# A two-layer hybrid block on one core: rows of v summed by column-quarter products, gates of both layers built through DRAM

## The chip, the cores and the metric

The kernel runs on one core of a Trainium2 chip. The metric is the device time of one execution in microseconds. Three runs of the kernel before are shown.

## What is computed

A block of two layers over 256 latent tokens and 256 context tokens of width 1024. Each layer mixes tokens (a gated delta rule in chunks, pooling, a Fourier mix), adds the result, and then retrieves experts. Context tokens go through the same weights, see only the context, and stop after the scan of the second layer. The change touches the retrieval:

```python
def _peer(h, w_query, sub_keys, expert_u, expert_v):
    ...
    best, pos = lax.top_k(cand.reshape(t, PEER_HEADS, PEER_TOPK * PEER_TOPK), PEER_TOPK)
    idx = jnp.take_along_axis(cand_idx..., pos, axis=-1)
    gate = jax.nn.softmax(best, axis=-1)
    ...
        act = jax.nn.gelu(jnp.einsum('td,thkd->thk', hb, expert_u[ib]), approximate=False)
        wgt = gb * act
        return jnp.einsum('thk,thkd->td', wgt, expert_v[ib])
```

Each token has 8 heads x 16 chosen experts of 16384 (128 x 128 keys). A chosen expert's row of u gives a score, its row of v is added with the weight gate times gelu(score).

## The kernel before

**Order of the work.** `_body` issues the parts in program order, and a scheduler of the tile framework then sets each engine's order; every engine works its own list strictly in that order. SP issues the loads of weights and tables, POOL the indirect fetches. The parts are: layer 0 of the context (`columns`, `scan`, `modulation`, `update`, `gather_select`), the latents of layer 0 (`columns`, `scan`, `update`, `dense_select`), the stream of layer 0, and layer 1 of the latents the same way. The second layer's scan of the context is `context()`, given to the stream of layer 0 for tile KV = 114.

**Two ways of retrieval.** For the latents all experts are worked out for all tokens (`stream`, line 1087). A tile is one first key, 128 experts. `first(i)` loads a tile of u, splits it in two parts (`hu` by ScalarE at line 1100, `lu` by POOL at line 231) and makes 24 products of 256 columns (lines 1111 to 1113); ScalarE applies gelu. `second(i)`, 17 tiles later in layer 0 and 32 later in layer 1, loads the tile of v, splits it (`hv`, and `lv` on VectorE at line 1101), multiplies the weights by the gates (line 1131), splits them too (`wh`, and `wl` on POOL in layer 0, on VectorE in layer 1), and makes 12 products of 512 columns (line 1142) into four banks.

**Gates.** They must lie as [second key, first key, token]. In layer 1 `build` (line 1059) makes one-hot masks of both keys for two tokens at a time (line 1070, VectorE), multiplies one by the gate (POOL or ScalarE), multiplies the two on TensorE (line 1082), and writes them to DRAM in 16 pieces of 1 MB; `second` reads 1 MB for every 8 tiles. In layer 0 `chunk` (line 1028) makes them within the stream, 32 first keys at a time: masks `two`, `one`, `og` on VectorE (lines 1037, 1041, 1046), and three bf16 products of 32 columns per token (line 1052).

**Rows of the context's experts.** For the context of layer 0 only the chosen rows are fetched. `gather_rows` (line 956) takes choice j of a block of 128 tokens: one indirect DMA from POOL brings [128, 2048], each token's row of u and of v side by side (line 966, 1 MB). VectorE multiplies the u half by the token and sums it (line 975, and every seventh later one on POOL and ScalarE), ScalarE makes the weight (lines 979, 980), and VectorE adds the v half times the weight (line 986). There are 256 such fetches, four buffers for the first 100 and three after. The first 100 are issued ahead of the latents of layer 0, the others by `context()`:

```python
    fetching = gather_rows(0, CTX, m, rows, buffer, chosen)
    for _ in range(UVN):
        next(fetching)
...
    sums = stream(0, keys, Hh, Hl, su, sv, LAG[0], {KV: context})
```

`modulation(0, (5,))` stands between scan and update of the latents; a vector of it is 16 products whose outputs are a quarter of the columns each, in groups of four side by side (`tile_position`), and 4.2 MB of weights.

Of the kernel before, what the change touches and what calls it, by code (L numbers as in the profile page):

```python
# [10 lines left out]
BF = mybir.dt.bfloat16  # L11
# [17 lines left out]
def _constants():  # L29
# [4 lines left out]
    # cumulative sums along the tokens of a chunk, forwards and backwards: [j, i]  # L34
# [5 lines left out]
    # masks are added to exponents' arguments: [token, token], nothing outside a chunk  # L40
# [55 lines left out]
def _layout(i):  # L96
# [25 lines left out]
    for l in range(depth):  # L122
# [22 lines left out]
def _body(st, tc, a, out, dbg, until):  # L145
# [26 lines left out]
    # the banks of PSUM: three for projections, one for each of three chains, two that sum outputs  # L172
# [3 lines left out]
    KC, TC = 32, 8  # first keys of a chunk of gates, tokens at a time  # L176
# [14 lines left out]
    class Stage:  # L191
        """tiles of a pool that is opened and closed by hand"""
# [11 lines left out]
    def bank(shape, tag):  # L204
        tag = roles.get(tag, tag)
        if tag == "pj":
# [26 lines left out]
    def rsqrt(x, n, tag=""):  # L233
        """1 / sqrt(x) of [128, n] positive values, by Newton's steps."""
# [10 lines left out]
    def two_parts(x, hi, lo):  # L245
        """x as a sum of two parts that the tensor engine reads exactly in one pass each"""
# [4 lines left out]
    def product(out, x, y, start, stop):  # L251
        """out += x^T y, of operands in one part, or in two: only the product of the two second ones drops out"""
# [4 lines left out]
    def wtile(name, *index):  # L257
        """2048 of a weight's columns as two tiles; a function of a row of 128 and the columns' width"""
# [43 lines left out]
    def scales(l, which, m, s):  # L302
        """norm's weight times 1 + scale, and the shift: [128, 8] each"""
# [4 lines left out]
    def in_rows(vec, half, tag):  # L308
        """half of [128, 8] as a row of 512, the same on all partitions"""
# [10 lines left out]
    def normed(x, xn, tag, scratch=None):  # L320
        """xn = x / rms(x), by rows"""
# [7 lines left out]
    def transposed(xns, sc, sh, hT):  # L329
        """hT [128, 8, 256] = (xn * sc + sh) transposed"""  # L330
# [16 lines left out]
    def columns_by_feature(name, c, hs):  # L347
        """256 columns of a weight times hT: [128, 2, 256], a column per partition"""
# [10 lines left out]
    def columns_by_token(name, n, h):  # L359
        """512 columns of a weight times hT: a block's [128, 512] each, a token per partition"""  # L360
# [33 lines left out]
    spots = cp.tile([128, NKEYS, TC], BF, tag="spots", name="spots")  # L394
    dve.tensor_copy(spots, iota[:, :, None].to_broadcast([128, NKEYS, TC]))
# [9 lines left out]
    def columns(l, s, m, full, keep, tl):  # L405
# [4 lines left out]
        else:  # the last use of X  # L410
# [13 lines left out]
        # gates of the delta rule: [token, block, 16]  # L424
# [16 lines left out]
        # softplus(z) = max(z, 0) + ln(1 + exp(-|z|))  # L441
# [24 lines left out]
        # factors by token: [beta, -beta exp(g), exp(g_end - g)]  # L466
# [6 lines left out]
        # decay of a whole chunk, on all partitions: [chunk, 8]  # L473
# [13 lines left out]
        def conv(part, hp):  # L487
            """silu of the short convolution for two heads: part 0, 1, 2 = q, k, v: [128, 2, 256]"""
# [814 lines left out]
```

## Time and profile before

| what | us |
|---|---|
| three runs: median, lowest, highest | 3429.58, 3420.82, 3435.34 |
| the profiled execution: its span, the one time that the page gives of it | 3421.3 |
| busy in it: TensorE products / weight loads | 2934.5 / 2488.9 |
| busy: VectorE, ScalarE, POOL | 2721.9, 1407.8, 1658.3 |
| DMA engines: moved, mean rate | 712.74 MB, 208 GB/s |

The span runs from the first to the last instruction. A busy share over the span mixes stages with different limits, so the stages are read one by one. Products are pipelined, so a busy TensorE need not be at its peak; the granted clock is 1 at 2.4 GHz and 0.5 at 1.2 GHz, and means in between mix the two. A product of fp32 operands shows as two records. "Idle before" names what ended the wait.

### The profile page before, as it was taken

Reading aid. Unit: us, or ns where it says so; the run is one execution under the profiler, and the core shown is the slowest. Engines: PE = TensorE matmul, PEld = TensorE weight load, DVE = VectorE, ACT = ScalarE, POOL = GpSimd, SP = SyncE. Lnnn points to the kernel's source line nnn. Section 1 sums busy time; section 2 is a strip of 40 time slices with the busy share of each in tenths; the row PEclk is TensorE's granted clock in tenths of the full one; section 3 lists DMA queues with packets and bytes.
Section 4 is the critical chain, followed back from the end, with each engine's and each line's share of the span. In section 5 each row is a group of like instructions: output and inputs, shape, how many; then the busy total and the mean of one; then the engine's idle time right before and its main releaser. Section 6 shows DMA issues by size and latency. Waiting matters only on the chain. (4 is left out here: it accounts for less than half of the span.)

```text
span 3421.3 us, 51677 instructions
## 1 busy us (share of the span) xinstructions
PE 2934.5 (86%) x19512; PEld 2488.9 (73%) x19512; DVE 2721.9 (80%) x4617; ACT 1407.8 (41%) x2648; POOL 1658.3 (48%) x976
## 2 busy tenths in 40 slices
PE   7999946768497898898899799999776899999998
PEld 4687725636386787787788677878576788899997
DVE  4535999879999999999999976643399967777777
ACT  4533334222233443344344354643235834444443
POOL 0241237732555775777677542334256732344442
PEclk9999967879687997999899899999889999999999
DMA  6603875688666876877677653252243576666664
GB/s 249 221 26 133 334 287 211 225 345 297 233 222 240 288 252 216 283 258 268 235 275 267 227 185 114 70 174 87 65 127 111 185 245 204 198 211 212 211 209 136
DMA packets 192106, 712.74 MB, mean 208 GB/s; under 512 B 18544, under 2 KB 58864, under 8 KB 157040
## 3 DMA queue, kind: packets, MB, share of 16 engines
q1 hardware_dynamic: 154992, 440.98, 38.9%
q0 software_dynamic: 36864, 268.45, 21.7%
q8 instruction: 153, 2.51, 0.3%
q14 instruction: 97, 0.79, 0.1%
HBM read 690.49 MB, written 18.87 MB: 207 GB/s over the span
## 5 line engine op out<-in xcount | busy, mean ns | idle before, releaser
L231 POOL TENSOR_TENSOR lu<-w,hu 128x1024 fp32r<-128x1024 f32 x256 | 670.5, 2619 | 512.0 <-ACT hu L1100 498.1
L1111 PE MATMUL s<-Hh,hu 128*128 128x256 f32 x2048 | 607.9, 297 | 75.4 <-ACT we L1115 63.0
L1113 PE MATMUL s<-Hh,lu 128*128 128x256 f32 x2048 | 604.2, 295 | 21.3 <-POOL lu L231 20.7
L966 POOL DMA_INDIRECT uv<-in_uv,idx x256 | 378.1, 1477 | 483.1 <-DVE acc L986 265.7
L1112 PE MATMUL s<-Hl,hu 128*128 128x256 f32 x2048 | 596.7, 291 | 0.0
L1111 PEld LDWEIGHTS s<-Hh,hu 128*128 128x128 f32 x2048 | 411.6, 201 | 93.0 <-ACT we L1115 72.2
L1113 PEld LDWEIGHTS s<-Hh,lu 128*128 128x128 f32 x2048 | 410.4, 200 | 28.3 <-POOL lu L231 26.9
L986 DVE SCALAR_TENSOR_TENSOR acc<-uv,dots,acc 128x1024 f32<-128x1024 f32 x254 | 409.9, 1619 | 14.7 <-ACT dots L980 14.5
L1112 PEld LDWEIGHTS s<-Hl,hu 128*128 128x128 f32 x2048 | 409.9, 200 | 6.9 <-issue 0.4
L1101 DVE TENSOR_TENSOR lv<-w,hv 128x1024 fp32r<-128x1024 f32 x256 | 356.3, 1392 | 59.6 <-ACT hv L1100 58.4
L1100 ACT CAST hu<-w 128x1024 fp32r<-128x1024 f32 x256 | 268.0, 1047 | 277.0 <-PE s L1112 206.6
L1131 DVE TENSOR_TENSOR we<-we,g 128x256 f32<-128x256 f32 x128 | 258.4, 2034 | 145.0 <-ACT we L1115 126.0
L975 DVE SCALAR_TENSOR_TENSOR uv<-uv,h 128x1024 f32<-128x1024 f32 x237 | 349.6, 1477 | 14.7 <-DMA uv<-in_uv,idx 14.5
L1100 ACT CAST hv<-w 128x1024 fp32r<-128x1024 f32 x256 | 267.9, 1046 | 213.8 <-PE pj L1142 169.3
L1052 PE MATMUL c<-og,two 128*128 128x32 bf16 x3072 | 234.5, 243 | 59.2 <-DVE og L1046 56.6
L1052 PEld LDWEIGHTS <-two 128*128 128x128 bf16 x3072 | 209.1, 160 | 95.0 <-issue 47.4
L979 ACT ACTIVATE dots<-dots 128x1 f32<-128x1 f32 x256 | 51.8, 203 | 519.1 <-DVE uv L975 518.5
L231 POOL TENSOR_TENSOR wl<-we,wh 128x256 fp32r<-128x256 f32 x128 | 146.5, 1146 | 122.9 <-ACT wh L1133 73.2
L1142 PE MATMUL po<-lv,wh 128*128 128x512 f32 x512 | 172.2, 418 | 29.5 <-DVE lv L1101 28.8
L1142 PE MATMUL po<-hv,wh 128*128 128x512 f32 x512 | 167.1, 407 | 15.7 <-ACT hv L1100 8.8
L231 POOL TENSOR_TENSOR C<-L,levels 128x512 f32<-128x512 f32 x96 | 135.2, 1424 | 86.9 <-PE c L665 38.1
L1142 PE MATMUL po<-hv,wl 128*128 128x512 f32 x512 | 164.3, 402 | 3.3 <-POOL wl L231 3.3
(427 smaller groups left out, 6433.3 us busy)
## 6 DMA issues: line engine op xcount, KB each, us to landing
w<-in_tab SPq DMA_DIRECT2D x512, 512.0 KB, 4.5
w<-in_wmod SPq DMA_DIRECT2D x96, 512.0 KB, 5.1
w<-in_wq SPq DMA_DIRECT2D x48, 512.0 KB, 4.6
w<-in_win SPq DMA_DIRECT2D x44, 512.0 KB, 4.7
gd<-gs SPq DMA_DIRECT2D x16, 1024.0 KB, 4.3
g<-gd SPq DMA_DIRECT2D x16, 1024.0 KB, 5.8
w<-in_wrest SPq DMA_DIRECT2D x24, 512.0 KB, 3.8
w<-in_wout SPq DMA_DIRECT2D x24, 512.0 KB, 4.9
```

The costliest lines, as they stand in the source:

```text
L231: pool.tensor_tensor(out, x, y, op=op)
L966: pool.indirect_dma_start(out=uv, out_offset=None, in_=a[f"uv{l}"], in_offset=bass.IndirectOffsetOnAxis(ap=st["idx", b][:, j0 + i : j0 + i ...
L975: dve.scalar_tensor_tensor(uv[:, 0:D], uv[:, 0:D], 1.0, st["h2", b], op0=OP.mult, op1=OP.mult, accum_out=dots[:, i : i + 1],)
L986: dve.scalar_tensor_tensor(acc, v, dots[:, i : i + 1], acc, op0=OP.mult, op1=OP.add)
L1052: pe.matmul(p[:, t1 - t0 + t], two[:, :, t], og[:, i, :, t], start=(i == 0), stop=(i == 2))
L1100: act.copy(hi, raw)
L1101: eng(lo, raw, hi.bitcast(F32), op=OP.subtract)
L1111: pe.matmul(p, hi[:, ks], Hh[:, k], start=(k == 0), stop=False)
L1112: pe.matmul(p, hi[:, ks], Hl[:, k], start=False, stop=False)
L1113: pe.matmul(p, lo[:, ks], Hh[:, k], start=False, stop=(k == KT - 1))
L1131: dve.tensor_tensor(wt, wt, g, OP.mult)
L1142: pe.matmul(acc[b][n], x[:, ts], y[:, n * 512 : n * 512 + 512], start=(i == 0 and j == 0), stop=(i == NKEYS - 1 and j == 2),)
```

## The change

1. The table `uv0` becomes two, `u0` and `v0`. A fetch brings [128, 1024], 512 KB, into one of eight buffers. There are 512 of them.
2. The rows of u are fetched as before, a choice of 128 tokens at a time, and their scores go to one column each. The gelu, the gates and a transposition follow once per block of 128 tokens.
3. The rows of v are fetched the other way: the 128 chosen rows of one token, a row per partition. A product sums them: the stationary operand `wz` is [128, 32], zero but for the token's own column. Two tokens and two halves of the 1024 columns take the four column quarters of the array. After 64 tokens ScalarE copies the bank, and two DMAs from ScalarE's queue put it in place of h2.
4. All u of the first block come first; then u of the second block and v of the first take turns; then the rest of v. The first 256 are issued ahead of the latents of layer 0, the others at tile 8 of the stream (`REST`), no longer in `context()`.
5. `chunk` goes. `build` serves both layers: masks `two` of four tokens at a time, and `one` with the gate in one VectorE operation per token. In layer 0 it stands ahead of the stream.
6. `modulation(0, (5,))` moves into the context's `modulation(0, (2, 4, 3, 5))`.

```diff
-            a[f"uv{l}"] = np.concatenate([i["expert_u"][l], i["expert_v"][l]], 1)
+            a[f"u{l}"], a[f"v{l}"] = i["expert_u"][l], i["expert_v"][l]
...
-    KV = 114
+    KV, REST = 114, 8
...
+    def gather_rows(l, s, m, rows, st):
+        pairs, half = 32, 64
+        wz = rows("wz", [128, half, pairs])
+        pool.memset(wz, 0.0)
+        spots_of = wz.rearrange("p (g r) c -> p g (r c)", g=2)[:, :, 0 : pairs * pairs : pairs + 1]
...
+        def fetch(table, index):
+            t = rows("uv", [128, D], ROWS)
+            pool.indirect_dma_start(
+                out=t, out_offset=None, in_=a[f"{table}{l}"], in_offset=bass.IndirectOffsetOnAxis(ap=index, axis=0)
+            )
+            return t
...
+        def scores(b):
+            dots = rows("dots", [128, HEADS * TOPK])
+            for j in range(HEADS * TOPK):
+                u = fetch("u", st["idx", b][:, j : j + 1])
+                dve.scalar_tensor_tensor(
+                    u, u, 1.0, st["h2", b], op0=OP.mult, op1=OP.mult, accum_out=dots[:, j : j + 1]
+                )
+                yield
+            act.activation(dots, dots, AF.Gelu)
...
+        def sums(b):
+            for q in range(128 // half):
+                t0 = q * half
+                dve.tensor_copy(spots_of, w_t[b][:, t0 : t0 + half].rearrange("p (g r) -> p g r", g=2))
+                p = bank([128, 512], "vb")
+                for r in range(pairs):
...
+                        vs.append(fetch("v", st["idx_t"][:, t : t + 1]))
...
+                    for n in range(2):
+                        for g in range(2):
+                            o = 32 * (2 * n + g)
+                            pe.matmul(
+                                p[o : o + 32], wz[:, g * pairs + r], vs[g][:, n * 512 : n * 512 + 512],
+                                start=(r == 0), stop=(r == pairs - 1), tile_position=(0, o),
+                            )
...
+    ROWS, EARLY = 8, 256
...
+                two = bp("two", [128, 4, 128], 3)
+                dve.tensor_tensor(
+                    two, chosen[:, 1, t0 : t0 + 4, None].to_broadcast([128, 4, 128]),
+                    iota[:, None, :].to_broadcast([128, 4, 128]), OP.is_equal,
+                )
+                one = bp("one", [128, 4, 128], 3)
+                for t in range(4):
+                    key, gate = (chosen[:, i, t0 + t : t0 + t + 1] for i in (0, 2))
+                    dve.tensor_scalar(one[:, t], iota, key, gate, op0=OP.is_equal, op1=OP.mult)
+                    pe.matmul(p[:, t], two[:, t], one[:, t], start=True, stop=True)
...
+    gd = gdram()
+    build(keys, gd, "right", ("c0", "c1"))
...
+    with using(vb="c2"):
+        sums = stream(0, gd, Hh, Hl, su, sv, LAG[0], {REST: fetch_rest, KV: context})
```

What the scheduler makes of it is read from the order of the built program. The first place is POOL's list in the stream of layer 0, near tile 40. Before, one fetch of 1 MB, one `lu` and one `wl` per tile:

```order
L966 DMA uv_16873<-in_uv,idx_2409 128x2048
L231 TENSOR_TENSOR lu_9312<-w_9309,hu_9311 128x1024
L966 DMA uv_16880<-in_uv,idx_2409 128x2048
L231 TENSOR_TENSOR wl_9460<-we_8514,wh_9457 128x256
L231 TENSOR_TENSOR lu_9367<-w_9364,hu_9366 128x1024
L966 DMA uv_16887<-in_uv,idx_2409 128x2048
L231 TENSOR_TENSOR wl_9515<-we_8569,wh_9512 128x256
```

With the change, four fetches of 512 KB per tile (`in_v` is the table of v, `idx_t` the choices by token):

```order
L231 TENSOR_TENSOR lu_10349<-w_10346,hu_10348 128x1024
L231 TENSOR_TENSOR wl_10497<-we_9547,wh_10494 128x256
L971 DMA uv_8541<-in_v,idx_t_2453 128x1024
L971 DMA uv_8543<-in_v,idx_t_2453 128x1024
L231 TENSOR_TENSOR lu_10404<-w_10401,hu_10403 128x1024
L971 DMA uv_8549<-in_v,idx_t_2453 128x1024
L971 DMA uv_8551<-in_v,idx_t_2453 128x1024
L231 TENSOR_TENSOR wl_10554<-we_9602,wh_10551 128x256
L971 DMA uv_8557<-in_v,idx_t_2453 128x1024
```

POOL issues twice the bytes per tile, and there are none left after tile 61; of the 512, 272 (200 of u, 72 of v) stand ahead of the first `lu` of the stream, where 110 of the 256 stood before.

The second place is TensorE's list around the start of the context's second layer (line 336 transposes its two blocks, `x_2` and `x_3`). Before, it stands by the last tile of u of layer 0:

```order
L1142 MATMUL pj_1571_6614<-hv_19412,wl_19419 128x512
L1142 MATMUL pj_1572_6615<-hv_19412,wl_19419 128x512
L336 MATMUL c_3297_17650<-ident,x_2_85 128x128
L336 MATMUL c_3298_17657<-ident,x_2_85 128x128
L1111 MATMUL s_6616<-Hh_5644,hu_19270 128x256
L1112 MATMUL s_6616<-Hl_5645,hu_19270 128x256
```

With the change it stands by tile 64 of u, and the scan that follows stands among the tiles up to the last (line 1133 is now the product with v, 1107 and 1108 those with u):

```order
L336 MATMUL c_3081_14590<-ident,x_2_85 128x128
L336 MATMUL c_3081_14590<-ident,x_3_87 128x128
L336 MATMUL c_3082_14597<-ident,x_2_85 128x128
L1107 MATMUL s_7630<-Hh_5795,hu_11784 128x256
L1108 MATMUL s_7630<-Hl_5796,hu_11784 128x256
```

The context's columns and scan have moved ahead by some 60 tiles, from behind the stream into it.

The third place is TensorE's list in the latents' `columns` of layer 0, where the first products of rows of v stand (line 1007). The first group stands together; in the second another part's products come between its first quarter and the rest:

```order
L1007 MATMUL s_3759<-uv_3760,wz_3361 32x512
L1007 MATMUL s_3759<-uv_3765,wz_3361 32x512
L1007 MATMUL s_3759<-uv_3760,wz_3361 32x512
L1007 MATMUL s_3759<-uv_3765,wz_3361 32x512
L592 MATMUL c_1132_4781<-t_1128_4772,t_1108_4710 128x256 x4
L1007 MATMUL s_3759<-uv_3774,wz_3361 32x512
L573 MATMUL c_1123_4758<-band_4759,t_1108_4710 64x128 x2
L573 MATMUL c_1123_4758<-band_4763,t_1108_4710 64x128 x2
L600 MATMUL c_1134_4788<-fy_4786,fw_4776 128x256 x2
L577 MATMUL c_1127_4769<-py_4767,wpool_1122_4756 128x256
L1007 MATMUL s_3759<-uv_3779,wz_3361 32x512
```

Such groups stand all along the list: 36 of the 128 come ahead of tile 1 of the stream, the other 92 among tiles 1 to 61, which is behind 240 of the fetches.

## Rows read from the trace of the kernel before

**Rows 1.** Stages: length, us busy (x instructions) by engine, clock, DMA share, GB/s.
```profile
0.00:310.00 310.00, 270.99 (x1746) 204.48 (x1747) 138.39 (x345) 127.91 (x256) 65.73 (x63) 0.95 0.44 150
310.00:890.00 580.00, 418.63 (x2004) 309.44 (x2002) 534.97 (x1511) 185.56 (x490) 252.62 (x172) 0.82 0.76 280
890.00:1468.00 578.00, 477.36 (x3763) 424.99 (x3764) 551.39 (x623) 225.09 (x442) 380.83 (x206) 0.87 0.71 246
1468.00:2010.00 542.00, 478.64 (x3638) 418.26 (x3637) 506.43 (x505) 231.80 (x440) 381.26 (x204) 0.92 0.73 250
2010.00:2130.00 120.00, 113.38 (x614) 94.20 (x613) 71.06 (x141) 58.61 (x109) 29.84 (x30) 1.00 0.45 140
2130.00:2457.00 327.00, 303.69 (x2152) 247.81 (x2150) 166.53 (x316) 142.75 (x283) 120.85 (x90) 0.98 0.33 104
...
2601.00:2740.00 139.00, 112.32 (x871) 104.37 (x870) 130.67 (x128) 116.99 (x223) 102.68 (x79) 0.99 0.48 171
```

**Rows 2.** VectorE, 310 to 890: xcount | busy us, mean ns | idle before.
```profile
L986 DVE SCALAR_TENSOR_TENSOR acc<-uv,dots,acc 128x1024 f32<-128x1024 f32 x106 | 157.9, 1497 | 5.2 <-ACT dots L980 5.1
L975 DVE SCALAR_TENSOR_TENSOR uv<-uv,h 128x1024 f32<-128x1024 f32 x109 | 150.7, 1386 | 13.2 <-DMA uv<-in_uv,idx 13.0
```

**Rows 3.** Groups of instructions, 890 to 1468.
```profile
L231 POOL TENSOR_TENSOR lu<-w,hu 128x1024 fp32r<-128x1024 f32 x63 | 172.0, 2731 | 50.4 <-ACT hu L1100 38.1 <-issue 8.0 <-ACT dots L979 3.9
L1111 PE MATMUL s<-Hh,hu 128*128 128x256 f32 x513 | 159.0, 310 | 37.9 <-ACT we L1115 25.5 <-DVE mod L294 11.7 <-ACT hu L1100 0.6
...
L966 POOL DMA_INDIRECT uv<-in_uv,idx x80 | 118.8, 1485 | 127.8 <-DVE acc L986 85.4 <-DVE one L1041 18.0 <-DVE best L779 5.4
```

**Rows 4.** The same stages, the fetches of line 966 alone.
```profile
310.00:890.00 580.00, 149.80 (x110) 0.82 0.76 280
```

**Rows 5.** The fullest 100 us of the DMA engines.
```profile
700.00:800.00 100.00, 69.41 (x238) 46.17 (x239) 85.09 (x194) 23.62 (x71) 39.95 (x27) 0.81 0.91 348
```

**Rows 6.** POOL's timeline, two places: start, us, instruction, [idle before].
```profile
330.93 0.94 POOL L966 DMA_INDIRECT uv<-in_uv,idx  x1 [0.31 <-issue]
...
580.79 1.78 POOL L966 DMA_INDIRECT uv<-in_uv,idx  x1 [0.16 <-PE c L665]
```

**Rows 7.** Groups of instructions, 2760 to 3390, the last stream.
```profile
L1111 PE MATMUL s<-Hh,hu 128*128 128x256 f32 x798 | 225.8, 283 | 0.0
...
L1142 PE MATMUL pj<-hv,wh 128*128 128x512 f32 x246 | 77.7, 396 | 0.0
```

**Rows 8.** The page's costliest groups, POOL's second parts of the weights.
```profile
L231 POOL TENSOR_TENSOR wl<-we,wh 128x256 fp32r<-128x256 f32 x128 | 146.5, 1146 | 122.9 <-ACT wh L1133 73.2
```

**Rows 9.** TensorE's timeline, the first transposes of four parts.
```profile
44.65 0.66 PE L336 MATMUL c<-ident,t 128*128 128x128 f32 x4
...
285.01 0.69 PE L336 MATMUL po<-ident,h 128*128 128x128 f32 x2 [6.10 <-DVE h L326]
...
2130.46 0.44 PE L336 MATMUL po<-ident,t 128*128 128x128 f32 x2
...
2456.69 0.66 PE L336 MATMUL c<-ident,xn 128*128 128x128 f32 x2 [8.77 <-DVE rsy L242]
```

**Rows 10.** DMA issues: size, median us from issue to landing.
```profile
w<-in_tab SPq DMA_DIRECT2D x512, 512.0 KB, 4.5
...
gd<-gs SPq DMA_DIRECT2D x16, 1024.0 KB, 4.3
...
uv<-in_uv,idx POOLq DMA_INDIRECT x256, 7.4
```

**Rows 11.** Groups over the whole run: the gates' build, and a tensor-scalar operation.
```profile
L1070 DVE TENSOR_TENSOR oh<-chosen,iota 128x512 f32<-128x512 f32 x128 | 130.7, 1097 | 1.2 <-ACT chosen L1017 1.2
...
L1082 PE MATMUL c<-oh 128*128 128x128 f32 x512 | 69.7, 283 | 23.0 <-ACT gs L1083 21.4 <-ACT oh L1078 0.8 <-POOL oh L231 0.7
...
L496 DVE TENSOR_SCALAR y<-xpad,convw 128x256 f32<-128x256 f32 x44 | 17.8, 441 | 16.7 <-ACT xpad L492 16.6
```

**Rows 12.** TensorE's timeline: quarter products of the modulation.
```profile
846.73 1.12 PE L284 MATMUL po<-w,cvec 128*32 128x512 f32 x8
```

More of the change, by code (lines that the diff above doesn't have):

```diff
@@ L912, in gather_select @@
         idx = rows("idx", [128, NB, HEADS * TOPK], 1, I32)
+        idx_t = rows("idx_t", [128, T], 1, I32)
         gate = rows("gate", [128, NB, HEADS, TOPK])
         st = {}
-        for b in range(NB):
-            st["acc", b] = rows(f"acc{b}", [128, D])
         sc, sh = scales(l, 1, m, s)
@@ L938, in after @@
                 by_token()
[L939 to L942 removed]
+            for t in (idx, idx_f):
+                dve.scalar_tensor_tensor(
+                    t[:, :, h * TOPK : h * TOPK + TOPK], keys[0][:, :, 0], float(NKEYS), keys[0][:, :, 1],
+                    op0=OP.mult, op1=OP.add,
+                )
         keys = [None]
+        idx_f = sp("idx_f", [128, NB, HEADS * TOPK])
         select(l, sp, (hT,), pair, lambda h, n: gate[:, :, h : h + n], GROUPS, after)
+        p = bank([128, T], "c2")
+        for b in range(NB):
+            pe.transpose(p[:, b * 128 : b * 128 + 128], idx_f[:, b], ident)
+        dve.tensor_copy(idx_t, p)
         for b in range(NB):
@@ new lines, in gather_rows @@
+    def gather_rows(l, s, m, rows, st):
[3 more added lines that the diff above has]
+        spots_of = wz.rearrange("p (g r) c -> p g (r c)", g=2)[:, :, 0 : pairs * pairs : pairs + 1]
+        w_t = {}
+        def fetch(table, index):
[8 more added lines that the diff above has]
+                u = fetch("u", st["idx", b][:, j : j + 1])
+                dve.scalar_tensor_tensor(
+                    u, u, 1.0, st["h2", b], op0=OP.mult, op1=OP.mult, accum_out=dots[:, j : j + 1]
+                )
+                yield
+            act.activation(dots, dots, AF.Gelu)
+            dve.tensor_tensor(dots, dots, st["gate", b].rearrange("p h k -> p (h k)"), OP.mult)
+            p = bank([128, 128], "vb")
+            pe.transpose(p, dots, ident)
+            w_t[b] = rows(f"w_t{b}", [128, 128])
+            act.copy(w_t[b], p)
+        def sums(b):
[4 more added lines that the diff above has]
+                for r in range(pairs):
+                    vs = []
+                    for g in range(2):
+                        t = b * 128 + t0 + g * pairs + r
+                        vs.append(fetch("v", st["idx_t"][:, t : t + 1]))
+                        if g == 0:
+                            yield
+                    for n in range(2):
+                        for g in range(2):
+                            o = 32 * (2 * n + g)
[3 more added lines that the diff above has]
+                            )
+                    if r < pairs - 1:
+                        yield
+                o = rows("sum", [128, 512], 2)
+                act.copy(o, p)
+                for n in range(2):
+                    act.dma_start(
+                        st["h2", b][t0 : t0 + half, n * 512 : n * 512 + 512], o[n * half : n * half + half]
+                    )
+                yield
+        yield from scores(0)
+        first = sums(0)
+        for _ in scores(1):
+            yield
+            next(first)
+            yield
+        for _ in first:
+            yield
+        yield from sums(1)
+        residual(l, s, m, [[st["h2", b][:, n * 512 : n * 512 + 512] for n in range(2)] for b in range(NB)])
@@ L1017, in dense_select, with build @@
             act.copy(chosen[:, :, b * 128 : b * 128 + 128], p)
[L1018 to L1024 removed]
         sp.close()
         return Hh, Hl, chosen
[L1028 to L1059 removed]
+    def build(chosen, gdram, side, banks):
         bp = Stage("build", side)
@@ L1171, in _body @@
     with using(c2="s", pj="s"):
-        modulation(0, (2, 4, 3))
+        modulation(0, (2, 4, 3, 5))
     cu = Stage("update", "right")
@@ L1183, in _body @@
     cw.close()
-    def buffer():
-        n = buffer.n
-        buffer.n += 1
-        if n < UVN and n % (UVA + UVB) >= UVA:
-            return extra("uv", [128, 2 * D], UVB)
-        return steady("uv", [128, 2 * D], UVA)
-    buffer.n = 0
-    fetching = gather_rows(0, CTX, m, rows, buffer, chosen)
-    for _ in range(UVN):
+    fetching = gather_rows(0, CTX, m, rows, chosen)
+    for _ in range(EARLY):
         next(fetching)
-    extra.close()
     lk, lc = Stage("keep", "right"), Stage("columns", "right")
@@ L1203, in _body @@
     ls.close()
-    with using(c2="s", pj="s"):
-        modulation(0, (5,))
     lu = Stage("update", "right")
@@ L1216, in _body @@
         nc.sync.dma_start(xdram[b], X[LAT, b])
-    with using(c2="s", pj="po"):
+    with using(pj="po"):
         modulation(1, (1, 0))
@@ L1237, in context, with fetch_rest @@
         ck.close()
-    sums = stream(0, keys, Hh, Hl, su, sv, LAG[0], {KV: context})
+    def fetch_rest():
+        for _ in fetching:
+            pass
+    with using(vb="c2"):
+        sums = stream(0, gd, Hh, Hl, su, sv, LAG[0], {REST: fetch_rest, KV: context})
     with using(c2="s"):
@@ L1270, in _body @@
     gd = gdram()
-    build(1, keys, gd, "right")
+    build(keys, gd, "right", ("c0", "c1", "c2"))
     residual(1, LAT, m, stream(1, gd, Hh, Hl, su, sv, LAG[1]))
```

117 lines of the change are left out of this document (10 added, 107 removed).

## The prediction, written before the change was timed

> **What bounds the kernel now.** I read the stages first. The starts of the stages are the first products of each part: the first latent tile of tables at 890 us, tile 64 at 1468 (513 products with `hu` in that stretch are 64 tiles of eight, and one) [rows 1, 3], the last near 2010. From 310 to 2010 VectorE is busy 535 of 580 us, 551 of 578 and 506 of 542, while the products' clock is granted at 0.82 to 0.92 and the DMA engines stand at 0.71 to 0.76 [rows 1]. So VectorE sets the pace there, and the reader should see that no other engine is near its end. From 2010 to 2457 it is the opposite: VectorE 71 of 120 and 167 of 327, TensorE 113 of 120 and 304 of 327 at a clock of 0.98 to 1.00. There the context's last scan and the last layer's columns run side by side. The same work of columns, scan and update, without a second scan beside it, took 240 us in the first layer (first transposes at 44.65 us, those of the next part at 285.01) against 327 here (2130.46 to 2456.69) [rows 9]. From 2740 the last stream is bound by products: 798 products with `hu` are 99.75 tiles of u, and with as good as 123 tiles of v they fill 630 us, so half a tile (u or v) costs 630 / 223 = 2.83 us [rows 7].
>
> **The change, part by part.** All times are against the profiled execution, whose span is 3421.3 us; the median of the three runs shown is 8.3 us above it.
>
> *A, 0 to 310.* The modulation's vector 5 moves here: eight loads of 512 KB, 4.2 MB. The DMA engines stand at 0.44 there [rows 1]. Hidden it costs 0, exposed at the stage's 150 GB/s 28 us. I take 10, since the products it sits beside leave most of the queue free.
>
> *B, 310 to 890.* Before, 110 fetches of 1 MB were issued here [rows 4]; by the order, 272 of 512 KB now come ahead of the first latent tile, 200 of u and 72 of v. VectorE loses 106 sums of 1.50 us (158 us) and gains 91 more dots of 1.39 us (126 us) [rows 2]: -32. The DMA engines gain 272 x 0.524 - 110 x 1.049 = 27 MB and lose the 4.2 MB of A: 23 MB, 66 us at the 348 GB/s of the fullest stretch [rows 5], on top of 0.76 x 580 = 441, so 507 of 580. POOL has 253 us now [rows 1], of which 150 are fetches [rows 4]; a fetch costs it 0.94 + 0.31 us back to back and 1.78 + 0.16 beside VectorE's work on two operands [rows 6], so 272 are 340 to 528 us and POOL ends at 443 to 631. VectorE's relief is small, and two others come near. I take -10, with -40 (VectorE's 32 and some waits) and +60 (POOL's upper end, 51, and some waits) as the ends.
>
> *C, tiles 0 to 63, 578 us now.* The gates in chunks go, and with them VectorE's `two`, `one` and `og`, and the 1.50 us sums [rows 2]. What remains must be priced on three others.
> DMA: 240 fetches (126 MB), 64 tiles of u and 47 of v (58 MB), the gates to DRAM (16 x 1 MB [rows 10], 17 MB), six of their reads (6 MB), the rest 1: 208 MB. At 348 GB/s [rows 5] that is 598 us; at the 246 GB/s this stage moved while VectorE held it [rows 1] it is 846.
> POOL: 240 fetches at the stage's 1.485 + 0.15 (392), 64 `lu` at 2.73 (175) [rows 3], 47 `wl` at 1.15 (54) [rows 8]: 621. With the two prices of [rows 6] it is 527 to 695.
> TensorE: (64 + 47) x 2.83 = 314, the gates 70 [rows 11], and 92 groups of four quarter products. Such a group, eight records, took 1.12 us in the modulation [rows 12]; where the order puts another product between the quarters it may take twice that. So 103 to 206, together 487 to 590 at full clock, or 560 to 678 at this stage's 0.87.
> VectorE: 56 dots, the gates (121, under F), 47 pairs of `lv` and `we`: under 350. It is no longer the bound.
> Three sums lie at 598, 621 and 487 to 678, and every row passes through all three in program order, so one waits for another: I take 670, 12% over the DMA's own time, with 600 and 760 as ends.
>
> *D, tiles 64 to 127, 542 us now.* All rows are there by tile 61 in the order, and the context's columns and scan, before behind the last u tile, now stand among these. Products: 64 x 2 x 2.83 = 362, and the context's. TensorE is busy 113 + 304 us in E [rows 1]; less the 240 us of columns, scan and update and 17 tiles of v (48) that leaves 129 for the context, with waits between its small products. Packed between tiles they may take two thirds, 86 (an estimate). With 120 it is 482. I take 500, ends 448 and 560.
>
> *E, 2010 to 2457, 447 us now.* Left over: 17 tiles of v (48), the residual and the norm (20: the norm alone kept TensorE idle 8.77 us at 2456.69 [rows 9]), the 240 us of columns, scan and update, and 12 of the context's end that the order leaves here. 320; ends 290 (the scan wholly gone and the tail overlapped) and 400 (the last layer's four modulation vectors as long as now).
>
> *F, 2457 to the end.* Select stays, and the last 681 us too, since products bound them. The gates' build, 139 us [rows 1], changes: per four tokens two masks of 1.02 us (130.7 / 128 [rows 11]) become one, and four `one` of 128 elements come. For those the nearest row is 0.44 us for 256 elements [rows 11], so 0.22 to 0.44 each: 65 + 56 to 113 = 121 to 178 against 131 on VectorE, and the next two engines' parts in `one` go. TensorE is busy 112 of the 139, so little can be had. I take -15, ends -40 and +45.
>
> Sum: 10 - 10 + 92 - 42 - 127 - 15 = **-92**, a span of 3329 and a median of **3338 us**.
>
> **A rule against it.** The fetches are halved in size. Tile loads of 512 KB land 4.5 us after their issue, the rows' 1 MB 7.4 [rows 10], so per byte the small ones take a fifth longer, if nothing overlaps; with eight buffers in flight I count on the overlap that [rows 5] shows. The Trainium skill (DMA: Bandwidth & Descriptors, section Bandwidth) says to batch transfers to at least 1 MiB for 75% of the peak, and its section on one DMA's anatomy gives 2.0 us + bytes / 436e3, an estimate of 3.2 us for 512 KB. One after the other, C would by that be 768 us and the gain gone. The 110 fetches and the weights of stage B moved 280 GB/s, so they did not stand one after the other.
>
> **The rivals.**
> 1. *The fetches pace the stream* (slower). C's bytes move no faster than before, 246 GB/s: C = 846, the total 3514. (One at a time, at the 4.5 us of [rows 10], the fetches alone would be 1080.) For it: POOL's in-order queue, where a fetch stands behind `lu`, which waits for ScalarE's copy. Against: the 348 GB/s stretch. It decides from C = 762 on (273 GB/s), where nothing is gained. 0.13.
> 2. *The context only moves.* Its chain of small products waits in program order among the tiles, and TensorE idles with it: D = 560, E = 360, together +100: 3438, no change. For it: each level of the scan needs POOL, behind an `lu` of 2.73 us [rows 3]. Against: TensorE has two independent halves of a tile to put between. 0.11.
> 3. *Only products bind C.* C = 600, and B gives 40: 3238. For it: VectorE's two-operand work, which makes fetches long, is nearly gone after tile 30. 0.16.
> That the change is not done as it says is excluded by the order: fetches, gates and context stand where the text puts them.
>
> **How the numbers follow.** Forecast (3250 to 3410) 0.60. A measurement can tell 0.5% here, 17 us: faster below 3412 is the forecast and rival 3, 0.76; same is rival 2, 0.11; slower is rival 1, 0.13. The range 3240 to 3450 takes in the forecast, rival 2, half of rival 3, and the lower part of rival 1: the terms' ends, added in squares, are some -90 and +115 about 3338.
>
> **What would show it.** Right: tile 64 near 1560, the context's columns before the last u tile, tile 127 near 2060, the last layer's first transposes near 2140 and its select 240 us on, DMA over 300 GB/s and VectorE under 70% from 890 to 1560. Wrong: a clock under 0.7 in C with TensorE waiting for `uv`; POOL over 95% busy in B with the first tile after 950; a last layer that still takes 327 us from its transposes to its select.

## The result and the profile after

The changed kernel takes 3451.97 us (median of five runs, 3438.91 to 3460.65) beside 3429.58 of the kernel before (3420.82 to 3435.34): a ratio of 1.0062, 95% interval 1.004 to 1.0085. It is slower by 22 us, where the forecast was 3338; the time lies 2 us above the upper end of the range. The profiled execution has a span of 3451.0 us.

First the places, as in [rows 9]: line 336 of the changed kernel, its TensorE instructions grouped by what is transposed, with the first and the last start.

```profile
L336 PE MATMUL c<-ident,t x32: 272/408/477, 12.2 to 509.6; 128*128 128x128 f32 x32
...
L336 PE MATMUL c<-ident,xn x32: 272/420/477, 865.6 to 2495.6; 128*128 128x128 f32 x32
...
L336 PE MATMUL po<-ident,h x16: 420/421/478, 297.1 to 302.3; 128*128 128x128 f32 x16
...
L336 PE MATMUL c<-ident,x x16: 270/272/273, 1693.1 to 1728.2; 128*128 128x128 f32 x16
...
L336 PE MATMUL po<-ident,t x16: 273/422/477, 2221.1 to 2229.0; 128*128 128x128 f32 x16
```

The rows read: the context's select begins at 297.1 (285.0 before), the latents' select of layer 0 at 865.6, the context's second layer at 1693, the last layer at 2221.1 (2130.5 before). The first tile of u stands at 972.54, tile 64 at 1695. The stages between them, to be held against [rows 1]: length, us busy by engine (PE, PEld, VectorE, ScalarE, POOL, with instructions), clock, DMA share, GB/s.

```profile
297.00:500.00 203.00, 86.58 (x354) 69.20 (x354) 173.83 (x701) 18.41 (x40) 112.62 (x89) 0.68 0.67 235
500.00:866.00 366.00, 311.17 (x1527) 186.16 (x1528) 245.60 (x469) 80.69 (x191) 275.75 (x224) 0.92 0.83 295
866.00:973.00 107.00, 87.34 (x440) 62.92 (x438) 96.18 (x520) 19.11 (x37) 35.93 (x27) 0.96 0.81 287
973.00:1695.00 722.00, 612.82 (x3453) 410.52 (x3453) 359.58 (x604) 228.17 (x315) 465.05 (x364) 0.92 0.86 298
1695.00:2221.00 526.00, 517.83 (x3322) 461.91 (x3320) 283.66 (x290) 270.79 (x418) 275.14 (x186) 1.00 0.51 166
2221.00:2491.00 270.00, 243.93 (x1612) 188.95 (x1612) 129.29 (x281) 114.39 (x230) 72.37 (x55) 0.95 0.37 125
...
2638.00:2790.00 152.00, 128.59 (x972) 124.52 (x972) 142.86 (x315) 84.58 (x103) 46.85 (x19) 0.92 0.50 176
```

Against the prediction's terms, in us of difference to the kernel before (A and B parted at the select's start, the forecast for D and E at the last layer's: -42 and 40 of E's 127):

| term | forecast | measured |
|---|---|---|
| A, to the context's select | +10 | +12 |
| B, from there to the first tile (605, now 676) | -10 | **+71** |
| C, tiles 0 to 63 (578, now 722) | +92 | +144 |
| D and E up to the last layer (662, now 526) | -82 | -136 |
| E, last layer up to its select (327, now 270) | -87 | -57 |
| F, the rest | -15 | -4 |
| sum | -92 | +30 |

C is 52 over and what follows 54 under: together the stream stands at +8 for a forecast of +10, and that the two errors cancel is luck. Of the 122 us that are missing, 81 lie in B, 30 in the last layer, 11 in F.

**What changed in B.** The same stretch, from the context's select to 500 us, before:

```profile
285.00:500.00 215.00, 170.58 (x763) 125.95 (x763) 194.09 (x742) 78.22 (x184) 59.28 (x42) 0.87 0.72 265
```

TensorE had 171 us of work beside the select, now it has 87 of 203 and its granted clock is a mean of 0.68. The work that stood there was the latents' `columns`: before, their transposes (`c<-ident,t`) ended at 295.9 us, with the select just begun; now they end at 509.6. VectorE's timeline of the changed kernel shows what they come behind (start, us, instruction):

```profile
485.30 0.42 DVE L949 CAST idx_t<-c 128x256 int32<-128x256 f32 x1
485.63 1.22 DVE L980 SCALAR_TENSOR_TENSOR uv<-uv,h 128x1024 f32<-128x1024 f32 x1
486.78 0.08 DVE L980 DVE_READ_ACCUMULATOR uv<-uv,h 128x1 f32 x1
486.78 0.21 DVE L324 TENSOR_SCALAR ss<-ss 128x1 f32<-128x1 f32 x2
```

Line 949 is the last step of the context's select, line 324 the first norm of the latents. The traces say the same of VectorE's 48 convolution operations of the latents' columns: in the kernel before all of them run ahead of the select's last index, in the change none does. The columns' pools open on the right side of the memory, the rows' pool and the select's on the left, and the change's rows (eight buffers, `wz`, two sums) take more of it. **Theory**: the pools no longer fit beside each other, the columns wait until the select's are closed, and that lost overlap is what B cost. **Rivals**: the 272 early fetches or the first sums by products made B long; or the stream's own pace (bytes, POOL's list, products) is what the forecast missed.

### The profile page after: what moved, and what is told of

It is laid out like the page before. It is cut to its first block, busy times and chain, and to the rows that moved or that the text cites. A ratio compares the mean times of both kernels' runs of the same rounds, so it can differ in the third digit from the quotient of the medians.

```text
span 3451.0 us, 48402 instructions
## 1 busy us (share of the span) xinstructions
PE 2990.6 (87%) x17980; PEld 2364.5 (69%) x17980; DVE 2171.7 (63%) x4539; ACT 1250.2 (36%) x1972; POOL 1666.0 (48%) x1150
## 3 DMA queue, kind: packets, MB, share of 16 engines
q10 hardware_dynamic: 640, 1.05, 0.1%
## 5 line engine op out<-in xcount | busy, mean ns | idle before, releaser
L231 POOL TENSOR_TENSOR lu<-w,hu 128x1024 fp32r<-128x1024 f32 x256 | 627.6, 2453 | 667.5 <-ACT hu L1096 623.6
L1122 DVE TENSOR_TENSOR we<-we,g 128x256 f32<-128x256 f32 x256 | 402.5, 1586 | 498.2 <-ACT we L1111 467.6
L971 POOL DMA_INDIRECT uv<-in_u,idx x256 | 311.4, 1216 | 155.8 <-issue 41.3
L971 POOL DMA_INDIRECT uv<-in_v,idx_t x256 | 282.1, 1102 | 193.3 <-PE c L1007 71.4
L1077 DVE TENSOR_SCALAR one<-iota,chosen 128x128 f32<-128x128 f32 x512 | 211.8, 477 | 0.0
L1111 ACT ACTIVATE we<-s 128x256 f32<-128x256 f32 x256 | 97.3, 380 | 244.9 <-PE s L1109 243.8
L1007 PE MATMUL c<-uv,wz 128*32 128x512 f32 x768 | 170.3, 633 | 17.7 <-DMA uv<-in_v,idx_t 17.4
L1079 ACT COPY gs<-c 128x512 f32<-128x512 f32 x128 | 129.6, 1061 | 137.1 <-PE c L1078 129.4
L1078 PE MATMUL c<-one,two 128*128 128x128 f32 x1024 | 147.6, 287 | 33.3 <-DVE one L1077 29.8
L231 POOL TENSOR_TENSOR wl<-we,wh 128x256 fp32r<-128x256 f32 x128 | 115.1, 899 | 121.5 <-ACT wh L1124 100.9
```

The lines of the kernel that those rows point to most:

```text
L231: pool.tensor_tensor(out, x, y, op=op)
L971: pool.indirect_dma_start(out=t, out_offset=None, in_=a[f"{table}{l}"], in_offset=bass.IndirectOffsetOnAxis(ap=index, axis=0))
L1007: pe.matmul(p[o : o + 32], wz[:, g * pairs + r], vs[g][:, n * 512 : n * 512 + 512], start=(r == 0), stop=(r == pairs - 1), tile_position=( ...
L1077: dve.tensor_scalar(one[:, t], iota, key, gate, op0=OP.is_equal, op1=OP.mult)
L1122: dve.tensor_tensor(wt, wt, g, OP.mult)
```

## The experiments

All places are read from line 336 as above. I is from the context's select to the latents' select of layer 0, II from there to the last layer's columns, III to its select, IV to the end. Ratios are to the kernel before, timed beside each run.

| kernel | median us | ratio, 95% interval | I | II | III | IV |
|---|---|---|---|---|---|---|
| before | 3429.58 | | 478 | 1367 | 326 | 965 |
| the change | 3451.97 | 1.0062, 1.004 to 1.0085 | 569 | 1356 | 269 | 960 |
| seven_buffers | 3382.05 | 0.9852, 0.9835 to 0.9868 | 483 | 1363 | 278 | 962 |
| seven_buffers_pad | 3416.75 | 0.9947, 0.9926 to 0.9967 | 555 | 1320 | 279 | 962 |
| before_pad | 3495.09 | 1.0194, 1.0169 to 1.0218 | 557 | 1384 | 300 | 963 |
| half_v | 3416.81 | 0.9961, 0.9944 to 0.9978 | 590 | 1301 | 268 | 960 |
| whole_groups | 3421.68 | 0.9967, 0.9951 to 0.9983 | 554 | 1331 | 269 | 961 |
| seven_whole | 3347.94 | 0.9748, 0.9724 to 0.9771 | 473 | 1340 | 275 | 964 |
| seven_whole_early_128 | 3411.84 | 0.9937, 0.9915 to 0.9959 | 455 | 1367 | 326 | 966 |
| seven_whole_old_build | 3369.76 | 0.9812, 0.9787 to 0.9838 | 475 | 1362 | 278 | 958 |
| six_whole | 3325.19 | 0.9682, 0.9663 to 0.9702 | 472 | 1298 | 294 | 961 |
| **lu_on_vector** | **3273.15** | **0.9529, 0.9511 to 0.9546** | 475 | 1271 | 273 | 960 |
| lu_on_vector_half_v | 3285.10 | 0.956, 0.9539 to 0.9581 | 476 | 1288 | 272 | 962 |
| six_lu_on_vector | 3303.87 | 0.9626, 0.9606 to 0.9647 | 471 | 1296 | 279 | 963 |

### The overlap given back, and taken away

```diff
# seven_buffers
-    ROWS, EARLY = 8, 256
+    ROWS, EARLY = 7, 256
# seven_buffers_pad: that, and
     cw = Stage("select_weights")
+    pool.memset(cw("pad", [128, 512]), 0.0)
# before_pad: the kernel before, with that line alone
```

> The changed kernel with seven buffers of rows instead of eight, 4 KB per partition less. By the order of the built program the latents' columns of layer 0 then stand among the context's select again (29 of their 39 convolution operations ahead of its last index), where the change has none. Theory, lost overlap: the first latent tile comes 50 to 80 us earlier than the changed kernel's 973 us (893 to 923), the rest of the run is as long as it was, and the time is 3370 to 3400. Rival, the 272 early fetches or the sums by products make that stage long: the first tile stays within 20 us of 973, and with one buffer less the time is 3440 to 3475.

> The changed kernel with seven buffers, and a tile of 2 KB per partition that nothing reads in the stage of the select's weights, which is closed when the select ends. By the order none of the latents' convolutions stands ahead of the context's last index, as in the change. Theory, lost overlap: the time goes back to the changed kernel's, 3440 to 3475, first tile at 955 to 990. Rival, the number of buffers is what the run before this one shows: the pad changes nothing, and both are within 10 us of each other.

> The kernel before, with a tile of 2 KB per partition that nothing reads in the same stage. Its fetches, sums and gates are as they were; by the order its latents' columns (30 convolution operations, all ahead of the last index before) now come behind the context's select. Theory, lost overlap: the first latent tile moves from 890 to 940 to 970, and the time is 50 to 80 us longer, 3480 to 3510. Rival, the overlap is worth little and the change's stage is long by its fetches or products: under 20 us longer, below 3450.

The latents' columns and select in the grouped rows of line 336, of seven_buffers and then of before_pad:

```profile
L336 PE MATMUL c<-ident,t x32: 272/300/476, 12.1 to 315.0; 128*128 128x128 f32 x32
...
L336 PE MATMUL c<-ident,xn x32: 272/421/477, 780.4 to 2426.6; 128*128 128x128 f32 x32
```
```profile
L336 PE MATMUL c<-ident,t x32: 272/421/477, 12.9 to 510.1; 128*128 128x128 f32 x32
...
L336 PE MATMUL c<-ident,xn x32: 272/421/477, 845.7 to 2534.4; 128*128 128x128 f32 x32
```

With 4 KB less the columns start at 299 us again, stage I is 86 us shorter, and the run is 70 us faster than the change. In the kernel before, 2 KB that nobody reads move the columns to 497 us, stage I from 478 to 557, the first tile to 978, and the run by 62 us: the same loss of stage I, without a fetch or a product of the change. That memory decides the overlap, and that the lost overlap makes stage I long, is shown in both kernels.

Three expectations missed. The first tile of before_pad comes at 978, later than the 940 to 970 expected. With seven buffers the first tile does not come at 893 to 923 but at 1001: the scores' bank "s" is lent to the early sums, whose last product there starts at 998.2. So by the prediction's own mark, the first tile, the stage gets no shorter (676 us in the change, 703 here), although the select comes 85 us earlier; the select is the better mark, and stage I is measured to it. And the pad in the changed kernel costs 35 us, not the 60 to 90 expected: stage I loses 72, but by the time of the latents' select 234 fetches are out instead of 180, and stage II gets 43 back. One buffer fewer is worth the other 35 (3452 to 3417) by itself, most of it in stage II; six_whole takes that up. So of the 70 us of seven_buffers about half are the overlap's.

### What paces the rows in the stream

```diff
# half_v: the table of v holds columns 0 to 511, fetches bring them, products take them twice;
# the right half of the context's sums is left out
-    a[f"u{l}"], a[f"v{l}"] = i["expert_u"][l], i["expert_v"][l]
+    a[f"u{l}"], a[f"v{l}"] = i["expert_u"][l], i["expert_v"][l][:, : D // 2]
...
-    vs[g][:, n * 512 : n * 512 + 512],
+    vs[g][:, 0:512],
# whole_groups; seven_whole has ROWS = 7 too
                     for n in range(2):
-                        for g in range(2):
+                        for g in (1, 0):
```

> The changed kernel, with the left half of the columns of v alone in its table of v: the 256 fetches of v bring 256 KB instead of 512, and the products take that half twice (the context's right half of the sums is left out). Fetches, products and POOL's instructions are as many as they were; some 48 MB of the 208 MB of tiles 0 to 63 go. Theory, those tiles are bound by bytes at some 310 GB/s: 722 us becomes 600 to 640 (products, busy for 613, come next), the time 3340 to 3370. Rival, POOL's issues or the products set the pace there: 700 to 722, the time 3430 to 3460.

> The changed kernel with one line's order turned: of the two tokens of a group of quarter products the second one's, which is fetched last, comes first. By the order of the built program 114 of the 128 groups then stand whole, where in the change 77 are broken into a lone first product and the other three; the latents' columns still come behind the context's select. In the trace of the change a lone product takes TensorE 0.98 us, the other three 0.99, and a whole group 1.00. Theory, from tile 0 to the context's end TensorE sets the pace and each broken group costs it one more microsecond: the time from the latents' select of layer 0 to the last layer's first transposes falls by 40 to 75 us, the total is 3375 to 3412. Rival, the bytes or POOL's fetches pace that stage: under 15 us, 3435 to 3460.

> Both edits: seven buffers of rows, so that the latents' columns stand among the context's select again, and whole groups of quarter products (126 runs of 4 or 8 in the order, none broken). Theory, the two costs lie in different stages and add up: 3382 less the 40 to 75 us of the whole groups, 3305 to 3345. Rival, with seven buffers TensorE is no longer what the rows' stage waits for, or POOL's pace is next: 3360 to 3385.

half_v: tiles 0 to 63 take 710 us (996 to 1706), which is what the rival had (700 to 722). But it is not the same work as in the change. POOL's last fetch of the change, then of half_v, and the start of half_v's second layer of the context:

```profile
1643.97 0.94 POOL L971 DMA_INDIRECT uv<-in_v,idx_t  x1 [0.30 <-issue]
```
```profile
1572.15 0.95 POOL L971 DMA_INDIRECT uv<-in_v,idx_t  x1 [0.30 <-issue]
...
L336 PE MATMUL c<-ident,x x16: 270/272/327, 1617.2 to 1665.2; 128*128 128x128 f32 x16
```

The fetches end 72 us earlier, and the context's second layer begins at 1617, among these tiles, where the change has it at 1693, beside tile 64. So the bytes are a part of the pace of the fetches, and the length of the 64 tiles does not decide between the two expectations. The total fell by 35, more than the rival allowed and less than the theory: stage II lost 55, and I grew by 21.

whole_groups rests on these lines of TensorE's timeline of the change, four quarter products being eight records (start, us, instruction, records):

```profile
1501.99 1.05 PE L1007 MATMUL c<-uv,wz 128*32 128x512 f32 x2
1502.96 0.50 PE L1133 MATMUL pj<-lv,wh 128*128 128x512 f32 x1
...
1505.72 1.06 PE L1007 MATMUL c<-uv,wz 128*32 128x512 f32 x6
...
1508.08 1.06 PE L1007 MATMUL c<-uv,wz 128*32 128x512 f32 x8
```

One product, three or four take the same microsecond, if they stand next to each other. Naming first the row that is fetched last keeps a group together. In the trace of the change 77 groups stand broken, some 75 us of TensorE's time. Of these 30 came back in the total; in the profiled run tiles 0 to 63, with 240 fetches among them as in the change, take 693 us (958.8 to 1651.3) instead of 722. With seven buffers, where 97 groups were broken, 34 came back (3382 to 3348). Both are less than expected: TensorE, busy for 613 of 722 us, did not set the pace alone. The two costs add up, as the theory for seven_whole had it, short of its range by 3 us.

```diff
# lu_on_vector: seven_whole, and
-            hi, lo = table(i, 0, "u", pool_tt, make_u)
+            hi, lo = table(i, 0, "u", pool_tt if l else dve.tensor_tensor, make_u)
# lu_on_vector_half_v: that with half_v's edits; six_whole and six_lu_on_vector: ROWS = 6
```

> As seven_whole, with the second parts of the tiles of u (lu) of layer 0 on VectorE instead of POOL. From 1200 to 1690 us seven_whole keeps POOL busy for 397 of 490 us, the gaps between its fetches come on top, and moves 331 GB/s; VectorE is busy for 216. POOL loses 2.4 us per tile. Theory, POOL's list paces the rows' stage: a fetch comes every 2.4 to 2.6 us instead of 2.86, the last one 60 to 100 us earlier, and the time falls by 15 to 50 us. Rival, the bytes do, at some 330 GB/s: the last fetch and the time stay within 15 us.

> As lu_on_vector, with the left half of the columns of v alone in its table (half the bytes of 256 fetches; the context's right half of the sums is left out). By the order the last rows are summed at tile 48 instead of 83. Theory, POOL's list paces the rows' stage: little more is had than lu_on_vector has, under 15 us. Rival, the bytes do: a fetch of v comes every 1.6 to 2.2 us, the last one is out before 1550, and TensorE's products alone are left: 20 to 60 us faster than seven_whole.

> As seven_whole, with six buffers of rows. By the order the last rows are summed at tile 102 instead of 83 and the context's second layer begins at tile 106 instead of 87. Theory, rows spread over more tiles leave TensorE less idle beside them, as long as the context still ends with the stream: tiles 0 to 63 take 20 to 50 us less, the total is between 10 us faster and 15 us slower than seven_whole, since the context now ends behind the stream. Rival, fewer buffers in flight slow every fetch: the last fetch is 60 or more us later, and the time is 20 to 60 us longer.

> As lu_on_vector, with six buffers of rows instead of seven. By the order the last rows are summed at tile 92 instead of 83, and the context's second layer begins at tile 96 instead of 86. In lu_on_vector the DMA engines are busy at 0.99 from 1000 to 1450 us and at 0.54 from 1690 to 1950. Theory, that stretch is now bound by bytes, and the same bytes over more tiles leave TensorE less idle: 5 to 25 us faster than lu_on_vector, 3248 to 3268. Rival, what six buffers gave beside POOL's long list was only the spreading of that list, and the later context comes out behind the stream: 0 to 25 us slower, 3273 to 3298.

The stretch 1200 to 1690, of seven_whole and then of lu_on_vector (columns as above):

```profile
1200.00:1690.00 490.00, 441.56 (x2685) 318.80 (x2684) 216.07 (x179) 160.07 (x240) 397.28 (x293) 0.97 0.94 331
```
```profile
1200.00:1690.00 490.00, 470.98 (x2967) 356.24 (x2966) 231.11 (x282) 187.45 (x280) 251.65 (x240) 0.99 0.95 347
```

Groups of instructions, 1200 to 1600, of seven_whole (VectorE's `lv`, POOL's `lu`), then of lu_on_vector:

```profile
L1097 DVE TENSOR_TENSOR lv<-w,hv 128x1024 fp32r<-128x1024 f32 x49 | 97.9, 1998 | 87.0 <-ACT hv L1096 54.5 <-PE c L1007 23.0 <-issue 4.9
...
L231 POOL TENSOR_TENSOR lu<-w,hu 128x1024 fp32r<-128x1024 f32 x46 | 110.0, 2407 | 0.5
```
```profile
L1097 DVE TENSOR_TENSOR lu<-w,hu 128x1024 fp32r<-128x1024 f32 x52 | 66.6, 1286 | 26.5 <-ACT hu L1096 25.7 <-issue 0.4
L1097 DVE TENSOR_TENSOR lv<-w,hv 128x1024 fp32r<-128x1024 f32 x52 | 63.2, 1231 | 18.6 <-ACT hv L1096 11.8 <-PE c L1007 3.5 <-issue 1.7
```

And what TensorE's products with `lu` waited for in that stretch (us in total, times, longest), in the same order:

```profile
PEld s L1109 <- POOL lu L231: 45.4, 22, 4.8
PE s L1109 <- POOL lu L231: 32.2, 19, 4.6
```
```profile
PEld s L1109 <- DVE lu L1097: 6.4, 7, 1.4
PE s L1109 <- DVE lu L1097: 2.4, 4, 0.8
```

In seven_whole `lu` starts without a pause (0.5 us of idle time before 46 of them) and TensorE waits for it. Moved, it costs VectorE 1.29 us instead of POOL 2.41; VectorE's own `lv` falls from 2.00 to 1.23; TensorE's waits for `lu` all but go. The last fetch is out at 1624 instead of 1701, as the theory had it, and the run is 75 us faster, half as much again as the theory's upper end. `lu` on POOL is thus what the stage paid for; how much of the 75 us is the earlier fetches, how much TensorE's own waits for `lu`, and how much the shorter `lv`, no run separates.

Half the bytes of v on top of that give no time (3285 beside 3273). POOL's last fetch of lu_on_vector, then that of lu_on_vector_half_v and its stretch 1200 to 1690:

```profile
1623.90 0.94 POOL L971 DMA_INDIRECT uv<-in_v,idx_t  x1 [0.30 <-issue]
```
```profile
1443.15 0.96 POOL L971 DMA_INDIRECT uv<-in_v,idx_t  x1 [2.73 <-PE c L1007]
...
1200.00:1690.00 490.00, 471.04 (x2847) 354.11 (x2845) 212.61 (x292) 207.33 (x316) 209.84 (x202) 0.98 0.71 231
```

The fetches end 181 us earlier, before the 1550 that the rival named: once POOL is relieved, the bytes pace the fetches. The run gains nothing by it; TensorE is busy for 471 of these 490 us with either size.

Six buffers gave 23 us with `lu` on POOL, more than the theory's 10, though the last fetch came at 1800 instead of 1701 as the rival had it (stage II 42 shorter, III 19 longer, the context's second layer at 1841 instead of 1751); with `lu` on VectorE they cost 31, more than the rival's 25. So the gain of a smaller ring may be that it stretched POOL's list over more tiles; that reading fits both pairs of runs, but no run changed the spreading alone.

### The context's place, and the build

```diff
# seven_whole_early_128
-    ROWS, EARLY = 7, 256
+    ROWS, EARLY = 7, 128
# seven_whole_old_build: line 1070's masks of both keys for two tokens, the gate on POOL or ScalarE
+                    oh = bp("oh", [128, 2, 2, 128], 6)
+                    dve.tensor_tensor(oh, chosen[:, 0:2, ts, None]..., iota..., OP.is_equal)
+                    if t2:
+                        pool_tt(oh[:, 0], oh[:, 0], chosen[:, 2, ts, None]..., op=OP.mult)
```

> As seven_whole, with 128 fetches instead of 256 ahead of the latents' layer. By the order the last rows are summed at tile 118 instead of 83, and the context's second layer begins at tile 121 instead of 87. Theory, the context's place in the stream is worth what it no longer adds behind it: the last tile of u to the last layer's select takes 40 to 90 us longer, while the stage of the latents' first layer becomes 0 to 40 us shorter with fewer fetches in it; together 10 to 60 us slower than seven_whole. Rival, the early fetches are what makes that first stage long and the context hides behind the stream anyway: 20 or more us faster than seven_whole.

> As seven_whole, with the gates of both layers built as the kernel before built those of layer 1: masks of both keys for two tokens in one operation of VectorE, the gate multiplied in on POOL and ScalarE in turn. In the trace of the change the four operations with the gate take 0.48 us of VectorE each and the build of the last layer 152 us from the select's end, against 139 before. Theory, VectorE's four small operations are the dearer form: the last layer's build is 8 to 20 us shorter, layer 0's as much or less, 10 to 30 us faster than seven_whole in all. Rival, POOL is busy with fetches in layer 0 and the old form waits for it there: layer 0 loses 10 to 40 us, and the total is the same or slower.

With 128 early fetches stage I is 18 us shorter and the first tile comes at 854, but the context's second layer begins at 1994 instead of 1751, III is 326 again, as in the kernel before, and the run is 64 us slower, a little more than the theory's 60. So the early fetches cost stage I little, and the context's place is worth what they buy. The old build is the dearer one: 6 us shorter in IV, 22 longer in II. There its masks take 53 us of POOL from 770 to 1300 us, and 176 fetches start in that stretch instead of seven_whole's 188, as the rival had it.

## Why the prediction was wrong, step by step

**B is the step that failed**: "VectorE's relief is small, and two others come near. I take -10". It priced instructions and bytes, and took for granted that the latents' columns would stay beside the context's select. Of the two "others", POOL was busy for 113 of 203 and 276 of 366 us, the DMA engines at 0.67 and 0.83: neither was the wall of the whole stage, though the DMA engines stood at 0.98 from 500 to 615. The mechanism was one the sum had no term for, memory: it decides whether the two parts can stand beside each other, and the order of the built program shows it at a place that the text did not look at. Stage I lost 91 us to the kernel before (478 to 569). The overlap given back shortens it by 86 (seven_buffers), taken away again it costs 72 there and 79 in the kernel before. In the total its price is 62 us in the kernel before and 35 in the changed one, where stage II gets a part back. With seven buffers the time is 3382, within the forecast's 3250 to 3410.

**C and D, the stream**, came out as forecast in the sum (+8 for +10) and with the right causes in the wrong weights. C had "ends 600 and 760" around 670 and took 722. VectorE is no longer the bound there, as forecast: busy for 360 of 722. But none of the three sums at 598, 621 and 487 to 678 set the 722 alone. POOL's 621 was too dear: it was busy for 465, since 240 fetches cost it 258 us (1.08 each) and not 392. It counted by its order, not by its sum: TensorE's products with `lu` waited for POOL for 50 us of these 722.

```profile
L1109 PE MATMUL s<-Hh,lu 128*128 128x256 f32 x512 | 158.3, 309 | 50.4 <-POOL lu L231 50.0
```

That "another product between the quarters" may double a group was right: 77 of the 128 groups, and whole_groups puts some 30 of C's 52 us on them. The rest of C was not divided: no run moved `lu` off POOL in the change itself. D gained more than said, since the context fits between the tiles: its second layer starts at 1693, and TensorE is busy for 518 of 526 us.

**E** was forecast at 240 us for the last layer, from a first layer with three vectors of the modulation; it took 270. With vector 5 moved there, the first layer's own stage takes 253 (44.3 to 297.1), so a fourth vector is 13 of those 30; the rest was not pursued. That the context no longer stands there gave 57; with it back (early_128) the stage is 326.

**F**: the build's stretch took 152 us for 139, but 101 more of TensorE's records stand in it, and the last stream after it, forecast to stay at 681, took 661: together 7 shorter, and the select 3 longer. The row of `one`, and the masks':

```profile
L1077 DVE TENSOR_SCALAR one<-iota,chosen 128x128 f32<-128x128 f32 x252 | 109.3, 493 | 0.0
...
L1070 DVE TENSOR_TENSOR two<-chosen,iota 128x512 f32<-128x512 f32 x63 | 42.9, 681 | 3.7 <-PE c L1078 3.6
```

109.3 us of busy time for 252 is 0.43 each, the upper end of "0.22 to 0.44"; the median of all 512 of the run is 0.335, the longest 5.4.

**The rivals.** The fetches did not pace the stream to 762 (C is 722); the context did not merely move; products alone did not bind. Slower had 0.13, given to one mechanism, and the loss came by another. The text's own sign of a wrong B, POOL over 95% busy with the first tile after 950, was half right: the tile is late, POOL is not busy.

**The range** was narrower than its own working. The terms' ends (A -10 and +18, B -30 and +70, C -70 and +90, D -52 and +60, E -30 and +80, F -25 and +60), added in squares, are -101 and +164 and not "some -90 and +115". By that the upper end is 3502 and the measured time lies below it, with B wrong all the same.

**The rule** on transfers of 1 MiB (the Trainium skill, DMA: Bandwidth & Descriptors, section Bandwidth) spoke against the halved fetches. No run here bears it out. The stretch 500 to 615 of the change, then 1000 to 1450 of lu_on_vector, with fetches and loads of 512 KB side by side:

```profile
500.00:615.00 115.00, 96.78 (x385) 63.66 (x389) 100.59 (x237) 30.88 (x76) 78.74 (x62) 0.93 0.98 372
```
```profile
1000.00:1450.00 450.00, 404.16 (x2558) 310.75 (x2557) 266.01 (x413) 165.67 (x236) 255.88 (x224) 0.97 0.99 361
```

The engines moved 372 and 361 GB/s at shares of 0.98 and 0.99, more than the 348 of [rows 5] with fetches of 1 MB.

## What to carry to other kernels

When a change alters what a stage keeps in memory, look at which parts of the program still stand beside each other in the order, before pricing any instruction: 2 KB too many cost the kernel before 62 us here. In a stage where several engines come close to the wall, ask which of them has work that another could do more cheaply; the list with mixed duties is the first to try: here moving `lu` to VectorE from POOL, which issues the fetches too, gave 75 us. And products that share the array should be made ready together, by letting the first one wait for the last operand: that gave 30 and 34 us here.

## What was not expected of the hardware

- A quarter product takes TensorE as long alone as four of them side by side: 1.05 us for 2 records, 1.06 for 6 or 8.
- VectorE's `lv` took 2.00 us beside POOL's `lu` of 2.41 and 1.23 without it. The Trainium skill (SBUF — State Buffer, section "SBUF: two separate sides") has VectorE operations with two inputs and POOL operations that read the memory lock each other out for a whole instruction; the trace agrees: of the 49 `lv` of seven_whole in that stretch, the 26 that overlap no `lu` or `wl` of POOL have a mean of 1.22 us, the other 23 one of 2.87.
- Halving the bytes of 256 fetches brought the last fetch forward by 72 us in the change and by 181 in lu_on_vector; the run gained 35 us in the first and nothing in the second.
